# The state space branch and the convolutions of a hybrid trunk, scheduled ahead of the projections that run beside them

## The chip, the cores and the metric

The kernel runs on one core of a Trainium2 chip, as one program. Its engines are TensorE (PE for matmuls, PEld for their weight loads), VectorE (DVE), ScalarE (ACT), GpSimd (POOL) and SyncE (SP, which only starts transfers). Each engine has an instruction list of its own, fixed when the program is built; the engines are held together by semaphores. The metric is the device time of one execution in microseconds (us). Before the change it is 1503.3 us, the median of 3 runs (1502.55 to 1503.54).

## What is computed

A backbone of two layers over 256 latent tokens behind 256 context tokens, 512 tokens of width 1024 in all, in fp32. A conditioning vector gives shifts, scales and gates ("modulation"). Layer 0 mixes tokens with two parallel branches, a long convolution of order 2 on 768 channels and a diagonal state space model (S5) on 256 channels; layer 1 with a gated linear recurrence. Behind each stands a mixture of 32 experts.

```
def ab_mixer(h_lat, h_ctx, w_in, w_out, filt, conv_w, conv_b, hy_bias, s5p, ctx_out):
    ...
    p_lat = h_lat @ w_in
    u_lat = s5_in(p_lat)
    st_lf = s5_scan(u_lat, lam_bar[0], b_bar[0], st_cf[:, -1], False)
    st_lb = s5_scan(u_lat, lam_bar[1], b_bar[1], st_cb[:, 0], True)
    ...
    y = jnp.concatenate([hyena_mix(p[..., :3 * HY_D], filt, conv_w, conv_b, hy_bias),
                         s5_readout(u, st_f, st_b, c_mat, d, glu_w, glu_b)], axis=-1)
    return y.astype(p.dtype) @ w_out

def hyena_mix(u3, filt, conv_w, conv_b, bias):
    ...
    z = x1 * fft_conv(v, kf[:, 0], bias[0])
    return x2 * fft_conv(z, kf[:, 1], bias[1])
```

The in projection `w_in` is 1024 x 2560, the out projection `w_out` 1024 x 1024, the modulation of each layer 1024 x 6144.

## The kernel before

**Two kinds of work in layer 0.** `layer0_mixer` (L1214) traces layer 0's mixer as a main chain with work beside it, the *fill*.

The main chain has three parts. `tables()` (L1343) makes the S5 tables. `s5_mixer` (L793) and `s5_glu` (L830) are the state space branch: `s5_input` (L847) transposes the inputs `uT` by way of `UT` into `U`; then for each of four quarters of the groups `s5_quarter_tables` (L725) makes `Gt`, `Gm`, `Hm` and `Km`, `s5_state` (L870) multiplies `U` by `Gm`, rotates and scans on DVE and leaves `prev`, and three products per group (`Km` with `U`, `Hm` twice with `prev`) give the output. `Km` is laid out by eight small transfers from `KX` that ACT issues (L776). `convs()` (L1370) is the long convolution: for each of six units of 128 channels `hyena_spectra` (L935) makes the filter spectra `K`, and `hyena_unit` (L1025) does two convolutions, each a transform on PE (`zv` by `dft`), a stretch on DVE and POOL (`Z`, `t`, `Z`, `yy`) and the inverse transform on PE (8 products of `yy` and `dft`), whose result `zv` or `yo` is the next step's input.

The fill is a list of jobs that `pipeline` (L1175) runs a few matmuls at a time. `Inputs` and `Channels` (L1061) do the in projection of 128 columns: 24 matmuls of 512 columns (three products of split weights `whi`, `wlo` and split `h`), whose weights are split beforehand by ACT (`whi`) and POOL (`wlo`). `Mods` (L1113) do 512 columns of the modulation (16 matmuls of `sc` by `w`, then 4 transposes). `Out` (L1135) does 128 columns of the out projection for some of the channel blocks; it may be traced only when those units are done. All of them use the two PSUM banks `in`. The first list holds 12 in-projection jobs (4 steps each) and 10 modulation jobs (1 step each), 58 steps; the second the in projection of convolution units 0 to 3, the rest of the modulation and 32 out-projection jobs. The jobs of units 0 and 1 wait until the pool `hyzb` is opened, which is after S5 (L1362).

**What sets the order.** `drive` (L226) takes a step of the main chain, which yields a gap in us, and then traces fill steps until their costs cover the gap. That makes the order of tracing. From it the framework's scheduler makes each engine's list: it plays the program through in a model of the chip, and whenever an engine is free there, it takes, of the instructions whose inputs are ready, the one that was traced first. `E.first()` (L143) is `tc.high_priority(None)`: instructions traced inside it count as if traced at the program's start. In regions under `manual_schedule` the named engines keep the order of tracing among the region's own instructions; L1351 to 1353 (the first fill steps and `tables()`) is such a region for PE, while L1356, 1357 and 1387 are in none.

`tables()` yields over 80 gaps, each of which draws at least one fill step as long as there are any. So all 58 steps of the first list are traced before the first instruction of `s5_mixer`, and none is left to be traced between the steps of `s5_mixer` and `s5_glu`; the second list starts with `convs()`.

**Behind layer 0's mixer** `moe` (L1702) loads the expert weights (96 MB a layer) into pools that reuse the memory of the convolutions, routes the tokens and runs the experts; then comes layer 1 in the same way. Most operations are recorded at the helpers' lines: L165 matmul, L169 transpose, L172 ACT, L175 copy, L178 two-input elementwise, L181 scalar_tensor_tensor, L191 weight loads.

Of the kernel before, what the change touches and what calls it, by code (L numbers as in the profile page):

```python
# [2 lines left out]

# [1 line left out]

# [217 lines left out]
        yield  # L223


def drive(main, fill):  # L226


    for gap in main:
        while gap > 0:  # L230
            c = next(fill, None)
            if c is None:
                break
            gap -= c
# [558 lines left out]
def s5_mixer(E, o, ycat, tabs, hp, tp, wp):  # L793

    inp = []
    for m in range(2):
        if m == 0:
            Gm = next(tabs)
        inp.append((yield from s5_input(E, o, m, o.uT[:, m], wp, tp)))
    for m in range(2):  # L800
        U, ud = inp[m]
        y = o.uT[:, m].rearrange("p (g c) -> p g c", g=8)
        for i in range(2):
            q = 2 * m + i
            if q:
                Gm = next(tabs)
                yield 1.2
            sl = slice(4 * i, 4 * i + 4)
            prev = s5_state(E, o, q, U[:, sl], Gm, wp)
            yield 5.0  # L810
            Hm, Km = next(tabs)
            yield 4.5
            b = E.bank("s5")
            for g in range(4):
                oo = b[:, g * 64:(g + 1) * 64]
                E.mm(oo, Km[:, g, :], U[:, 4 * i + g, :], True, False)
                E.mm(oo, Hm[:, 0, g, :], prev[:, 0, g, :], False, False)
                E.mm(oo, Hm[:, 1, g, :], prev[:, 1, g, :], False, True)
            E.tt(y[:, sl], b[:, :256].rearrange("p (g c) -> p g c", c=64), ud[:, sl], ADD)
            if i == 1:  # L820
                yield 0.7
                yield from s5_output(E, m, y, ycat, tp)
            if q < 3:
                tabs = s5_quarter_tables(E, o, q + 1, hp, tp)
                next(tabs)
                yield 3.8
    E.dump('ys5', ycat[:, 6:8])


def s5_glu(E, ycat, tp):  # L830
    gw = tp.tile([P, 2, 512], F32, tag="Gt", name="gw")
    E.SY.dma_start(gw, E.a['s5_glu_w'][0].rearrange("(k p) n -> p k n", p=P))
    yield 0
    glb = E.prm['glb']
    ag = []
    for m in (2, 3, 0, 1):
        b = E.bank("s5")
        for k in range(2):
            E.mm(b, gw[:, k, m * P:m * P + P], ycat[:, 6 + k, :], k == 0, k == 1)
        ag.append(b)  # L840
    for m in range(2):
        sg = tp.tile([P, 512], F32, tag=f"t{'xy'[m]}", name="sg")
        E.act(sg, ag[m], AF.Sigmoid, bias=glb[:, 2 + m:3 + m])
        E.stt(ycat[:, 6 + m, :], ag[2 + m], glb[:, m:m + 1], sg, ADD, MUL)


def s5_input(E, o, m, uT, wp, tp):  # L847

    UT = tp.tile([64, 8, 8, 16], F32, tag="Gt", name="UT")
    uv = uT.rearrange("p (c j) -> p j c", j=8)  # L850
    for h in range(2):
        b = E.bank("s5")
        for i in range(4):
            E.tr(b[:64, i * P:(i + 1) * P], uv[:, 4 * h + i, :])
        E.copy(UT[:, :, 4 * h:4 * h + 4, :].rearrange("p g j n -> p j g n"),
               b[:64].rearrange("p (j g n) -> p j g n", j=4, g=8))
    yield 1.5
    U = wp.tile([P, 8, 64], F32, name="U", bufs=2)
    b = E.bank("s5")
    for g in range(8):  # L860
        E.tr(b[:, g * 64:(g + 1) * 64], UT[:, g].rearrange("p j n -> p (j n)"))
    bv = b.rearrange("p (g c) -> p g c", c=64)
    E.act(U[:, :, 0:32], bv[:, :, 32:64], AF.Copy)
    E.act(U[:, :, 32:64], bv[:, :, 0:32], AF.Copy)
    ud = wp.tile([P, 8, 64], F32, name="ud", bufs=2)
    E.tt(ud, U, bcast(o.dcol[:, 8 * m:8 * m + 8], 2, 64), MUL, E.G)
    return U, ud
# [47 lines left out]
def s5_output(E, m, y, ycat, tp):  # L915
    E.act(y, y, AF.Gelu_apprx_tanh)
    yield 0.8
    YT = tp.tile([64, 8, 8, 16], F32, tag="Gt", name="YT")
    for h in range(2):
        b = E.bank("s5")  # L920
        for i in range(4):
            E.tr(b[:64, i * P:(i + 1) * P], y[:, 4 * h + i, :])
        E.copy(YT[:, :, 4 * h:4 * h + 4, :].rearrange("p j g n -> p g j n"),
               b[:64].rearrange("p (g j n) -> p g j n", g=4, j=8))
    yield 1.5
    b = E.bank("s5")
    for j in range(8):
        E.tr(b[:, j * 64:(j + 1) * 64], YT[:, j].rearrange("p g n -> p (g n)"))
    bv = b.rearrange("p (j s c) -> p s c j", j=8, s=2)
    yv = ycat[:, 6 + m, :].rearrange("p (s c j) -> p s c j", s=2, j=8)  # L930
    E.act(yv[:, 1], bv[:, 0], AF.Copy)
    E.act(yv[:, 0], bv[:, 1], AF.Copy)
# [242 lines left out]
def pipeline(jobs):  # L1175


    now, late = 0.0, []

    def settle():  # L1180
        for x in list(late):
            while x[0] <= now:
                d = next(x[1], None)
                if d is None:
                    late.remove(x)
                    break
                x[0] = now + d

    jobs = iter(jobs)
    cur = next(jobs, None)  # L1190
    prepared = False
    while cur:
        while not cur.ready():
            yield None
        if not prepared:
            cur.prep()
        nxt = next(jobs, None)
        prepared = False
        for cost in cur.mms():
            if nxt and not prepared and nxt.ready():  # L1200
                nxt.prep()
                prepared = True
            settle()
            now += cost
            yield cost
        late.append([now, cur.after()])
        cur = nxt
    while late:
        now = max(now, min(x[0] for x in late))
        settle()  # L1210
        yield 0.4


def layer0_mixer(E):  # L1214
    class O:
        pass
    o = O()
# [6 lines left out]
    with ExitStack() as l0:  # L1224
        E.psum(l0, "left", **{"in": (1, 2), "tr": (1, 1)})
        pl = l0.enter_context(E.pool("p_l0", 1))
        ycat = pl.tile([P, KD, T], F32, name="ycat")
# [8 lines left out]
        hp = E.hp = s5s.enter_context(E.pool("s5h", 1, "right"))  # L1236
        tq = E.tq = s5s.enter_context(E.pool("s5t", 1, "right"))
# [76 lines left out]
        def more():  # L1314
            yield from first
            yield from jobs
            yh.extend(p_h.tile([P, KD, T], F32R, tag=f"h{i}", name=f"yh{i}") for i in range(2))
            for ks in ((4, 5, 6, 7), (0, 1), (2,), (3,)):
                for i in range(8):
                    yield Out(E, feed, i, ks, yh, ycat, tmp, lambda ks=ks: done.issuperset(ks), tail if ks[0] == 3 else None)  # L1320
                if ks[0] in (4, 0):
                    yield between.pop(0)
                    yield between.pop(0)
# [16 lines left out]
        fill = pipeline(more())  # L1340
        tabs = s5_quarter_tables(E, o, 0, hp, tq)
# [11 lines left out]
            drive(tables(), fill)  # L1353
        s5a.close()
        wp = s5s.enter_context(E.pool("s5w", 1, "right"))
        drive(s5_mixer(E, o, ycat, tabs, hp, tq, wp), fill)  # L1356
        drive(s5_glu(E, ycat, tq), fill)
        done.update((6, 7))
        s5s.close()
        hys = ExitStack()  # L1360
# [1 line left out]
        with hys, E.pool("hyzb", 2, "right") as zb, E.pool("hyk", 2, "right") as kp, E.pool("hyt", 1, "right") as tp, \  # L1362
                E.pool("hyw", 2, "right") as wp:
            zp.update({u: zb for u in (0, 1)})
            E.dft = zb.tile([P, 8, P], F32, name="dft", bufs=1)
            E.SY.dma_start(E.dft, a['k_dft'])
            order = (4, 5, 0, 1, 2, 3)
            filt = {}

            def convs():  # L1370
                for _ in hyena_spectra(E, 4, hdn2, kp, tp, filt):
                    yield 3.0
                for i, u in enumerate(order):
                    if i == 5:
                        tags = {"wge": ("fw3", 512), "bge": ("win", 256), "wA": ("hw", 1024), "lT": ("so", 512)}
                        ends["r"] = Route(E, 0, T // P, E.mT[0], lambda nm: tp.tile([P, tags[nm][1]], F32, tag=tags[nm][0], name=nm))
                        ends["r"].prepare(E.bank("hs")[:, 0])
                    spec = hyena_spectra(E, order[i + 1], hdn2, kp, tp, filt) if i < 5 else iter(())
                    steps(spec, 1)
                    while ("x1", u) not in zt:  # L1380
                        next(fill)
                    yield from hyena_unit(E, u, *filt[u], zt["v", u], zt["x1", u], ycat, wp, spec)
                    done.add(u)
                    run(spec)
                    yield 0.5

            drive(convs(), fill)
            run(fill)
    E.dump('ycat', ycat)
    E.dump('x1', E.xT)  # L1390
# [736 lines left out]
```

## Time and profile before

| | us |
|---|---|
| median of 3 runs | 1503.3 |
| the profiled execution's own time | 1504.8 |
| its span, first to last instruction | 1502.9 |
| PE busy | 1284.4 (85%) |
| DVE, ACT, POOL busy | 809.8, 381.9, 381.4 |
| mean granted TensorE clock | 0.925 |

Layer 0's mixer takes the first 530 us: the first list of the fill runs until 163, S5 until 274, the convolutions until 506, the last out projections and the norm until 530. The first mixture of experts takes 530 to 870. In the profile a busy PE at granted clock 1.0 runs at 2.4 GHz, at 0.5 at 1.2 GHz; a stretch with a mean between had both. Times in rows are us from the span's start.

### The profile page before, as it was taken

The page shows a single profiled execution, that of the slowest core. Times are in us where ns is not written, and L with a number is a line of the kernel's source. Part 1 is how long each engine was busy: PE and PEld are TensorE (multiplying, and loading weights), DVE is VectorE, ACT ScalarE, POOL GpSimd, SP SyncE. Part 2 cuts the span into 40 slices and gives each one's busy share as a digit, 9 for nine tenths or more (in the row PEclk, how much of TensorE's full clock was granted, in tenths as well). Part 3 has the DMA queues.
Part 4 walks back from the last instruction along what each step waited for, and adds up shares of the span by engine and source line. Part 5 has one row for each costly group of instructions (what it writes and reads, how often), then busy time and mean ns, then how long its engine had stood idle before and what let it go on. Part 6 is the DMA issues. An engine that isn't in the chain of part 4 may idle for free. (4 is left out here: it accounts for less than half of the span.)

```text
span 1502.9 us, 18344 instructions
## 1 busy us (share of the span) xinstructions
PE 1284.4 (85%) x6921; PEld 823.2 (55%) x6921; DVE 809.8 (54%) x1828; ACT 381.9 (25%) x644; POOL 381.4 (25%) x268
## 2 busy tenths in 40 slices
PE   5799698998888749999999487979798959999995
PEld 1566476566655433444444177878787733444443
DVE  4973364477776462444334687474747463444433
ACT  2323232222222321111111242333333212222211
POOL 0343343124544521111100342323232121111001
PEclk9899788898988869999999788999999979999998
DMA  9357533323032089999996102030303279999980
GB/s 380 148 197 281 201 122 95 124 74 120 14 111 84 29 333 379 412 384 372 380 388 239 65 8 113 29 112 29 113 28 120 96 316 376 417 418 417 419 330 31
DMA packets 54591, 311.88 MB, mean 208 GB/s; under 512 B 13239, under 2 KB 18648, under 8 KB 23128
## 3 DMA queue, kind: packets, MB, share of 16 engines
q1 hardware_dynamic: 47032, 302.68, 50.8%
q0 software_dynamic: 4608, 6.30, 1.3%
q10 hardware_dynamic: 2848, 1.58, 0.5%
q8 instruction: 59, 0.97, 0.3%
q14 instruction: 44, 0.36, 0.1%
HBM read 315.77 MB, written 4.19 MB: 213 GB/s over the span
## 5 line engine op out<-in xcount | busy, mean ns | idle before, releaser
L165 PE MATMUL pg_t<-w,Xe 128*64 128x512 f32 x1024 | 228.8, 600 | 0.0
L165 PE MATMUL in_t<-h,whl 128*128 128x512 f32 (+1 forms) x768 | 146.6, 349 | 3.2 <-DVE h L175 2.4
L165 PEld LDWEIGHTS pg_t<-w,Xe 128*64 128x64 f32 x1024 | 71.1, 138 | 135.7 <-issue 131.1
L178 POOL TENSOR_TENSOR whl<-wraw,whl 128x2048 fp32r<-128x2048 f32 x20 | 93.5, 4680 | 175.3 <-ACT whl L172 175.3
L165 PEld LDWEIGHTS in_t<-h,whl 128*128 128x128 f32 x768 | 122.3, 197 | 20.9 <-POOL h L178 3.1
L165 PE MATMUL in_t<-h,whi 128*128 128x512 f32 x320 | 112.4, 431 | 17.0 <-ACT whi L172 7.8
L165 PE MATMUL py_t<-w,hid 128*64 128x512 f32 x512 | 119.1, 606 | 4.2 <-DVE yl L178 3.0
L181 DVE SCALAR_TENSOR_TENSOR sg<-sg,ws,pg_t 128x256 f32<-128x256 f32 x32 | 15.4, 480 | 181.2 <-ACT sg L172 181.2
L181 DVE SCALAR_TENSOR_TENSOR xT<-sc_t,mT,xT 128x256 f32<-128x256 f32 x204 | 90.3, 480 | 29.6 <-PE sc_t L165 28.1
L178 POOL TENSOR_TENSOR wlo<-w,whi 128x1024 fp32r<-128x1024 f32 (+3 forms) x51 | 74.1, 1458 | 126.8 <-ACT whi L172 119.3
L1547 POOL MEMSET Xg<- 128x1024 f32 x32 | 30.4, 958 | 297.4 <-PE ga_t L169 297.3
L165 PE MATMUL sc_t<-OT,yh 128*128 128x512 f32 (+1 forms) x256 | 90.7, 369 | 10.1 <-DVE xT L181 7.8
L165 PEld LDWEIGHTS in_t<-h,whi 128*128 128x128 f32 x320 | 62.7, 205 | 36.6 <-issue 9.3
L165 PE MATMUL sc_t<-OT,yl 128*128 128x512 f32 (+1 forms) x256 | 82.6, 338 | 0.0
L165 PEld LDWEIGHTS sc_t<-OT,yh 128*128 128x128 f32 x256 | 48.1, 188 | 54.1 <-issue 27.6
L165 PEld LDWEIGHTS py_t<-w,hid 128*64 128x64 f32 x512 | 34.1, 138 | 64.8 <-issue 55.9
L165 PE MATMUL in_t<-h,wlo 128*128 128x512 f32 x160 | 68.4, 427 | 1.2 <-POOL wlo L178 1.1
L172 ACT ACTIVATE yh<-py_t 128x1024 fp32r<-128x1024 f32 (+1 forms) x34 | 33.1, 973 | 121.0 <-PE py_t L165 121.0
L185 DVE TENSOR_SCALAR OT<-ht_t,ksq 128x512 fp32r<-128x512 f32 (+1 forms) x32 | 19.7, 617 | 81.5 <-PE ht_t L165 81.5
L172 ACT ACTIVATE sg<-pg_t 128x256 f32<-128x256 f32 x32 | 12.3, 384 | 195.6 <-PE pg_t L165 195.6
L172 ACT ACTIVATE whi<-w 128x1024 fp32r<-128x1024 f32 (+3 forms) x52 | 34.4, 664 | 103.4 <-PE in_t L165 83.2
L165 PE MATMUL at_t<-QA,X 128*128 128x128 f32 x224 | 37.2, 316 | 26.9 <-DVE QA L178 26.9
(411 smaller groups left out, 2378.0 us busy)
## 6 DMA issues: line engine op xcount, KB each, us to landing
w<-in_w_gu_dram SPq DMA_DIRECT2D x128, 1024.0 KB, 10.4
w<-in_w_dn_dram SPq DMA_DIRECT2D x64, 1024.0 KB, 10.2
w<-in_w_mod_dram SPq DMA_DIRECT2D x24, 2048.0 KB, 7.9
wraw<-in_w_in_dram SPq DMA_DIRECT2D x20, 1024.0 KB, 5.6
w<-in_w_in_dram SPq DMA_DIRECT2D x5, 2048.0 KB
w<-in_w_out_dram SPq DMA_DIRECT2D x2, 2048.0 KB
cwo<-in_w_out_dram SPq DMA_DIRECT2D x2, 2048.0 KB
rows<-hh SPq DMA_DIRECT2D x6, 512.0 KB, 2.6
```

The costliest lines, as they stand in the source:

```text
L165: self.TE.matmul(o, l, r, start=st, stop=sp)
L172: self.S.activation(o, i, f, **k)
L178: (e or self.V).tensor_tensor(o, x, y, op=op)
L181: self.V.scalar_tensor_tensor(o, x, s, y, op0=op0, op1=op1)
L185: (e or self.V).tensor_scalar(o, x, s1, None, op0=op0)
L1547: E.G.memset(X, 0.0)
```

## The change

`drive` gets a third parameter. Where it is given, each step of the main chain is traced inside `E.first()`, and the fill steps as before. Three of the four calls give it: S5, its gated output, and the convolutions; the call for `tables()` does not. Nothing that is computed changes, nor the order of tracing, nor any buffer.

```diff
-def drive(main, fill):
-
-
-    for gap in main:
+def drive(main, fill, E=None):
+
+
+    while True:
+        with E.first() if E else nullcontext():
+            gap = next(main, None)
+        if gap is None:
+            return
         while gap > 0:
             c = next(fill, None)
             if c is None:
@@ -1353,8 +1357,8 @@
-        drive(s5_mixer(E, o, ycat, tabs, hp, tq, wp), fill)
-        drive(s5_glu(E, ycat, tq), fill)
+        drive(s5_mixer(E, o, ycat, tabs, hp, tq, wp), fill, E)
+        drive(s5_glu(E, ycat, tq), fill, E)
@@ -1384,7 +1388,7 @@
-            drive(convs(), fill)
+            drive(convs(), fill, E)
             run(fill)
```

## Rows read from the trace of the kernel before

**Rows 1.** The page, parts 1 and 2: engines, and the granted clock in 40 slices.
```profile
PE 1284.4 (85%) x6921; PEld 823.2 (55%) x6921; DVE 809.8 (54%) x1828; ACT 381.9 (25%) x644; POOL 381.4 (25%) x268
...
PEclk9899788898988869999999788999999979999998
```
**Rows 2.** Windows of layer 0's mixer: stretch, length, busy by engine, PEclk, DMA, GB/s.
```profile
100.00:154.00 54.00, 53.86 (x326) 36.52 (x324) 19.50 (x44) 16.46 (x28) 20.27 (x14) 1.00 0.76 306
154.00:264.00 110.00, 88.92 (x601) 65.71 (x600) 51.42 (x92) 30.35 (x56) 39.88 (x27) 0.83 0.39 134
264.00:345.00 81.00, 73.83 (x316) 48.54 (x315) 50.98 (x109) 20.32 (x34) 23.61 (x16) 0.91 0.28 95
345.00:506.00 161.00, 128.85 (x572) 92.58 (x572) 108.84 (x223) 38.51 (x81) 71.36 (x61) 0.87 0.20 75
506.00:530.00 24.00, 20.31 (x125) 10.10 (x125) 9.35 (x27) 8.41 (x20) 13.97 (x16) 0.93 0.22 63
```
**Rows 3.** The same windows for PE's fill products alone (tile in_t).
```profile
100.00:154.00 54.00, 46.81 (x236) 1.00 0.76 306
154.00:264.00 110.00, 42.94 (x184) 0.83 0.39 134
```
**Rows 4.** Timeline of PE from 97 us: start, us, engine, line, operation, count.
```profile
98.25 0.60 PE L169 MATMUL s_t<-ksq,uT 128*64 128x128 f32 x4
...
105.43 1.92 PE L165 MATMUL in_t<-w,sc 128*32 128x512 f32 x16
107.28 0.65 PE L169 MATMUL s_t<-ksq,uT 128*64 128x128 f32 x4
...
143.77 1.55 PE L165 MATMUL s_t<-U,Gm 128*128 128x64 f32 x12
```
**Rows 5.** Timeline of POOL: the last Hm product of the first quarter.
```profile
104.37 1.29 POOL L178 TENSOR_TENSOR Hm<-ux,uy 128x512 f32<-128x512 f32 x1
```
**Rows 6.** Timeline of PE, first and second quarter's output (idle time before, releaser).
```profile
170.75 0.80 PE L165 MATMUL in_t<-h,whi 128*128 128x512 f32 x1 [7.35 <-ACT whi L172]
175.95 0.66 PE L165 MATMUL s_t<-U,Km 128*128 128x64 f32 x2 [4.40 <-DMA Km<-KX]
...
184.87 0.36 PE L165 MATMUL s_t<-Hm,wB 64*16 64x112 f32 x2
...
202.43 0.33 PE L165 MATMUL s_t<-U,Km 128*128 128x64 f32 x2
```
**Rows 7.** Timeline of ACT: transfers that ACT issues, and what stands behind them.
```profile
163.91 5.69 ACTq L777 DMA_DIRECT2D Km<-KX  x7
169.65 2.00 ACT L172 ACTIVATE whi<-w 128x1024 fp32r<-128x1024 f32 x2 [5.77 <-issue]
...
192.10 4.47 ACTq L777 DMA_DIRECT2D Km<-KX  x7
```
**Rows 8.** Timeline of DVE and POOL around 214 us.
```profile
213.41 0.68 DVE L178 TENSOR_TENSOR ty<-wB,PG 128x512 f32<-128x512 f32 x1
...
214.85 2.73 DVE L178 TENSOR_TENSOR tx<-wB,PG 128x512 f32<-128x512 f32 x1
...
214.62 2.41 POOL L178 TENSOR_TENSOR wlo<-w,whi 128x1024 fp32r<-128x1024 f32 x1 [1.68 <-ACT whi L172]
```
**Rows 9.** Timeline of PE in the last convolution unit.
```profile
481.02 1.19 PE L165 MATMUL pd_t<-yy,dft 128*128 128x256 f32 x2 [3.94 <-DVE yy L178]
...
490.36 0.59 PE L165 MATMUL pd_t<-yy,dft 128*128 128x256 f32 x2
...
500.44 3.56 PE L165 MATMUL pd_t<-yy,dft 128*128 128x256 f32 x8 [6.35 <-DVE yy L178]
```
**Rows 10.** Waits of PE from 264 to 506 us: total, times, longest.
```profile
PE pd_t L165 <- DVE yy L178: 13.3, 4, 6.3
```
**Rows 11.** Timeline of SP: routing weights, and expert weights behind the mixer.
```profile
441.53 0.58 SPq L1415 DMA_DIRECT2D wge<-in_moe_wg_dram  x1
...
466.64 61.94 SPq L1533 DMA_DIRECT2D w<-in_w_gu_dram  x4
```

More of the change, by code (lines that the diff above doesn't have):

```diff
@@ L1 @@
 import math
-from contextlib import ExitStack
+from contextlib import ExitStack, nullcontext
 import numpy as np
```

## The prediction

> **What bounds the kernel now.** I read the page first: PE is busy for 85% of the span, DVE, the next, for 54%, and its granted clock drops in places [rows 1]. A change to the order of layer 0's mixer can win only there, so the next view was the table of windows over that mixer. In 100 to 154 us PE is busy for 53.86 of 54 us at clock 1.00; in 154 to 264 for 88.92 of 110 at 0.83; from 264 to 506 for 202.7 of 242 at 0.91 and 0.87 [rows 2]. DVE reaches 68% at most, DMA is at 0.20 to 0.39 from 154 on. So the mixer is PE-bound while there is fill, and afterwards bound by the main chain's latency, with PE idle or slowed. Filtered to the fill's products, the first of these windows has 46.81 us of them in 54 and the second 42.94 in 110 [rows 3]: the fill is used up early.
>
> The timeline of PE shows why. In the dense stretch S5's pieces stand at 98.25, 107.28 and, three further ones left out, 143.77 us, about 9.1 apart, each directly behind a modulation product (such as the one at 105.43, 1.92 us long) [rows 4]. That is where the first list has nothing ready for a moment. The whole first list was traced before S5, so it goes first; S5 gets one slot a round. Its first quarter's output product comes at 175.95, after the list has ended, with PE waiting 7.35 and 4.40 us just before [rows 6].
>
> **The change part by part.** No instruction is added or removed; three drives move forward in the lists. I sum against the profiled execution, 1504.8 us; the median of the runs is 1.5 us less.
>
> *S5, seen from its own chain.* With priority its pieces take PE when their inputs are there. The earliest it can have its first Hm is when POOL has finished it, 104.37 + 1.29 = 105.7 us; that belongs to `tables()`, which gets no priority [rows 5]. From the first product on Hm to the output product the second quarter, which met little fill, took 202.43 - 184.87 = 17.6 us, including the Km transfers [rows 6]. So the first output product could stand at 105.7 + 17.6 = 123 instead of 176: 53 us. The later three quarters already had precedence, because what ran beside them was traced after S5, so they keep their pace and only move.
>
> On VectorE S5's two-input operations move into a stretch in which POOL splits weights. The row: a `tx` of the usual shape took 2.73 us beside a `wlo` of 2.41 that had begun 0.23 earlier, while the `ty` before it took 0.68 [rows 8]: 2.05 us lost. The 236 fill products from 100 to 154 us [rows 3] are about six projection jobs (24 each) with as many modulations (16 each), so six `wlo`: up to 12 us of the 53 may go, 41 remain. The Trainium skill, SBUF — State Buffer, section "Who interferes with whom", says that a VectorE instruction with two SBUF inputs and a GpSimd instruction that reads SBUF exclude each other, whichever starts first holding the shared ports; the trace agrees with this by the 2.73. By that rule the chain would give 41, without it 53; the sum below uses neither.
>
> *S5, seen from PE.* Moving S5 up doesn't make its products vanish. What can be won is PE's idle time, 110 - 88.92 = 21.1 us, plus the slow clock: a mean of 0.83 means that 34% of the 110 us, 37.4, ran at 1.2 GHz; at 81% busy that is 30.3 us of work that takes half as long at 2.4, 15.1 saved. Together 36.2. That is less than the 41, so I take it as the term, since in 100 to 154 the fill held PE at 99.7% and clock 1.00. From it go the stalls that ACT makes: for each quarter it issues eight Km transfers, seven of them in 5.69 or 4.47 us, and the fill's weight splits stand behind them (5.77 us of idle ACT before `whi`) [rows 7]. PE waited 7.35 for that at the first quarter, when it had nothing else [rows 6]; in the dense stretch a running job covers most of it. Bounds per quarter: 0 and 7.35; I take 0.8, the nearer end because two `in` banks hold a job ahead, so 3.2 for four. S5 term: 33.0.
>
> *The convolutions.* An inverse transform is eight products. In the last unit the first was cut up by out projections: from 481.02 to 490.36 + 0.59, 9.93 us; the second stood alone and took 3.56 [rows 9]. Twelve such groups exist (two per unit). With priority they run in one piece. The last unit is on the path that sets the end, since only the last block of out projections is behind it: 9.93 - 3.56 = 6.4 us, and the work that is pushed aside fits into the 6.35 us that PE waits before the second group. For the other units the gain lies between 0 (the fill displaced has to be done anyway) and PE's idle time and slow clock in 264 to 506: 39.3 us idle, and by the same arithmetic 6.6 and 16.8 of clock, 62.7. I take 0 for them, as the row of a group without fill before it is from the last unit. Convolution term: 6.4.
>
> *Transfers.* The moved steps also issue the Km transfers on ACT (32, counted above), the load of the gate weights, two loads for each unit's filter and four routing loads on SP. They pass the weight loads of the fill on SP. Each takes SP about 0.58 us [rows 11] and DMA is mostly idle there; if a weight load had to wait for one, 0.6 us of a ring with three tiles ahead: nothing. On POOL a quarter's `Hm` products (1.29 each) [rows 5] go ahead of `wlo`; that is in the bounds of the starved rival.
>
> *What is late next.* Everything behind the mixer moves with its end. The expert weights reuse the convolutions' memory: three more of the four loads that start at 466.64 wait until 528.6 for it [rows 11]; they follow the mixer, and no wait of theirs stands still. The 24 us from 506 to 530 stay.
>
> Sum: 33.0 + 6.4 = 39.4. 1504.8 - 39.4 = 1465.4 in a profiled execution, 1464 as a median.
>
> **The rivals.**
>
> *The fill is starved.* ACT and POOL serve S5 first, and PE waits for `whi` and `wlo` in every quarter as at 170.75: 4 x 7.35 = 29.4 us. Of the 36.2 + 6.4 there remain 13.2: 1490. For it: the ACT row with 5.77 us idle. Against: at the second quarter the same transfers cost PE no such wait.
>
> *More than PE's stage shows.* S5 wins its full 53 and the fill that is left over goes into the idle time of the convolutions, where the last unit and one more win 6.4 each: 53 + 13 = 66, 1437. For it: 39.3 us of idle PE there. Against: the port rows above.
>
> *It doesn't do what it says.* In the scheduler's model S5 was not ready earlier either, for the shared tiles `Gt`/`UT` hold it, or the lists come out in nearly the same order: 1503. For it: one buffer for both. Against: pieces exactly behind each modulation product are the mark of a low rank, not of a late input.
>
> *Slower: PE's list waits at its head.* One mechanism: a main product now stands in PE's list where the model has its input ready, with no fill in front; if DVE and POOL are later on the chip, all of PE's list waits. Where no fill stood before it, the last inverse group waited 6.35 us; four such groups together 13.3 [rows 9, 10]. If all twelve wait 5 us, that is 60, 46.7 more than now, against the 33 of S5: 14 slower, 1517. It decides from (33 + 13.3) / 12 = 3.9 us a group. The Trainium skill, PSUM — Partial Sum Buffer, section "Engine vs sequencer instructions", says that matmuls start and complete in program order; the 6.35 us agree, since out projections were traced behind. Against: most groups wait less now, and eight of twelve not at all, though fill is low in the convolutions already.
>
> **How the numbers follow.** Forecast 0.50 (its own range 1446 to 1482: 53 for 36 on one side, the stalls on the other), starved 0.18, more 0.10, nothing 0.07, slower 0.15. Predicted 1464. A range from 1436 to 1504 leaves out the slower case and the far end of "more", about 0.18. The measurement tells 0.2%, 3 us, from no change: faster 0.78, same 0.07, slower 0.15.
>
> **What would show it.** In the changed kernel's trace: the transposes of `UT` and the products of `U` and `Gm` before 115 us and no longer one per modulation product; `U,Km` first at about 123 to 135; the gated output at about 235 to 240 instead of 272; the fill's products in 154 to 264 rising from 43 towards 65 us and the clock there above 0.95; inverse groups of eight in one piece; the first large run of expert loads near 489 instead of 529. Wrong, if the first `U,Km` stays behind 160, if PE's wait for ACT `whi` or POOL `wlo` grows to over 20 us between 100 and 264, or if its waits for `yy` exceed 45 us: then the gain is eaten where the rivals say.

## The result, and the profile after

The changed kernel takes 1522.8 us (1520.9 to 1530.7) against 1503.2: ratio 1.0141 [1.0103, 1.0179], slower by 1.4%, where 1464 was predicted. Its profiled execution took 1524.7 us, span 1522.9. On the page, PE's busy time grew by 18.6 us with the same number of products [rows 1]; in the third and fourth of the 40 slices (76 to 152 us) the granted clock is 0.7 for 0.9.
```profile
span 1522.9 us, 18342 instructions
...
PE 1303.0 (86%) x6921; PEld 825.7 (54%) x6921; DVE 825.4 (54%) x1828; ACT 381.7 (25%) x644; POOL 380.2 (25%) x268
...
PEclk9977889899887878999999979999999979999998
```
The windows of the mixer, all engines:
```profile
100.00:154.00 54.00, 44.00 (x257) 27.57 (x256) 30.06 (x47) 13.29 (x28) 26.98 (x22) 0.78 0.36 127
154.00:264.00 110.00, 95.52 (x562) 61.36 (x560) 48.76 (x103) 29.62 (x49) 26.54 (x19) 0.91 0.41 153
264.00:345.00 81.00, 73.37 (x347) 53.15 (x347) 53.92 (x108) 20.52 (x33) 28.79 (x17) 0.94 0.37 137
345.00:506.00 161.00, 138.68 (x594) 96.74 (x593) 107.18 (x194) 37.25 (x72) 64.01 (x51) 0.86 0.23 83
506.00:530.00 24.00, 15.48 (x71) 8.21 (x68) 6.66 (x18) 9.42 (x25) 12.19 (x18) 0.86 0.46 175
```
The same windows for PE's fill products (tile in_t):
```profile
100.00:154.00 54.00, 21.64 (x81) 0.78 0.36 127
154.00:264.00 110.00, 48.27 (x220) 0.91 0.41 153
264.00:345.00 81.00, 43.09 (x179) 0.94 0.37 137
345.00:506.00 161.00, 75.41 (x299) 0.86 0.23 83
506.00:530.00 24.00, 13.10 (x53) 0.86 0.46 175
```
The dense stretch is gone: from 100 to 154 us there are 81 fill products for 236 and the clock is 0.78 for 1.00 [rows 2, 3]. The later windows make up for it bit by bit: 220 for 184, then 179 for 120, 299 for 248, and behind 506 us 53 for 24.

S5 did move. The timeline of PE (last field: idle time before, and who ended it) has the first quarter's products on Hm from 105, its output product at 128 (before: 175.95 [rows 6]), and pauses where S5 heads the list and GpSimd's Hm is not there:
```profile
105.31 0.56 PE L165 MATMUL s_t<-Hm,wB 64*16 64x112 f32 x8 [1.33 <-POOL Hm L178]
105.80 1.04 PE L165 MATMUL in_t<-w,sc 128*32 128x512 f32 x2
109.72 0.55 PE L165 MATMUL s_t<-Hm,wB 64*16 64x112 f32 x2 [2.88 <-POOL Hm L178]
...
114.51 3.43 PE L165 MATMUL in_t<-w,sc 128*32 128x512 f32 x14
...
128.32 0.41 PE L165 MATMUL s_t<-U,Km 128*128 128x64 f32 x2 [1.98 <-DMA Km<-KX]
...
137.68 0.36 PE L165 MATMUL s_t<-Hm,wB 64*16 64x112 f32 x2 [2.98 <-POOL Hm L178]
```
The second pause cuts a modulation in two: two of its 16 products run at 105.80, and the other 14, whose weights are there, only at 114.51, behind the wait for `Hm` and S5's products.

The end of the mixer, as ACT and DVE show it: the last unit's copy `yo`, the last two modulations' copies `ms`, and the multiplication that finishes a unit (`ycat`).
```profile
498.40 0.60 ACT L172 ACTIVATE yo<-pd_t 128x512 f32<-128x512 f32 x1 [8.28 <-PE pd_t L165]
...
506.11 0.60 ACT L172 ACTIVATE ms<-in_t 128x512 f32<-128x512 f32 x1 [1.01 <-PE in_t L165]
...
517.44 0.60 ACT L172 ACTIVATE ms<-in_t 128x512 f32<-128x512 f32 x1 [7.42 <-PE in_t L165]
...
520.30 0.88 DVE L181 SCALAR_TENSOR_TENSOR ycat<-tr_t,nv,ycat 128x256 f32<-128x256 f32 x2 [0.83 <-PE tr_t L169]
```
And PE in the same stretch, with SP's issue of the load that PE waits for:
```profile
448.08 3.23 PE L165 MATMUL pd_t<-yy,dft 128*128 128x256 f32 x8 [2.36 <-DVE yy L178]
...
504.12 1.92 PE L165 MATMUL in_t<-w,sc 128*32 128x512 f32 x16
...
506.10 0.33 SPq L191 DMA_DIRECT2D w<-in_w_mod_dram  x1
...
514.00 3.37 PE L165 MATMUL in_t<-w,sc 128*32 128x512 f32 x16 [5.55 <-DMA w<-in_w_mod_dram]
...
519.63 0.63 PE L169 MATMUL tr_t<-ksq,yo 128*128 128x128 f32 x4
...
537.77 0.40 PE L165 MATMUL in_t<-yh,wlo 128*128 128x512 f32 x1
```
`yo` is ready at 498.40 but is transposed at 519.63. Its transposes take the one `tr` bank, whose uses follow the order of tracing; the last modulations were traced earlier, so their transposes have it first. They are late: the last one's products wait 5.55 us for a weight load that SP issued at 506.10, as the products of the one before ended. Before, the modulations were done first, and the last `yo` went straight through:
```profile
476.26 0.60 ACT L172 ACTIVATE ms<-in_t 128x512 f32<-128x512 f32 x1 [2.09 <-PE in_t L165]
...
504.03 0.60 ACT L172 ACTIVATE yo<-pd_t 128x512 f32<-128x512 f32 x1 [10.17 <-PE pd_t L165]
...
505.46 0.88 DVE L181 SCALAR_TENSOR_TENSOR ycat<-tr_t,nv,ycat 128x256 f32<-128x256 f32 x2 [4.57 <-PE tr_t L169]
...
519.52 0.40 PE L165 MATMUL in_t<-yh,wlo 128*128 128x512 f32 x1
```
Behind the last out-projection product (519.5 before, 537.8 after) the rest of the span is 983.4 and 985.1 us: of the 20.0 us that the profiled span grew by, 18.3 are lost in the mixer.

### The profile page after: what moved, and what is told of

Read it like the earlier page. It is cut to its first block, busy times and chain, and to the rows that moved or that the text cites. A ratio compares the mean times of both kernels' runs of the same rounds, so it can differ in the third digit from the quotient of the medians.

```text
span 1522.9 us, 18342 instructions
## 1 busy us (share of the span) xinstructions
PE 1303.0 (86%) x6921; PEld 825.7 (54%) x6921; DVE 825.4 (54%) x1828; ACT 381.7 (25%) x644; POOL 380.2 (25%) x268
## 5 line engine op out<-in xcount | busy, mean ns | idle before, releaser
L165 PE MATMUL in_t<-w,sc 128*32 128x512 f32 x384 | 67.2, 696 | 8.4 <-DMA w<-in_w_mod_dram 8.4
```

The source lines that it names most:

```text
L165: self.TE.matmul(o, l, r, start=st, stop=sp)
```

## The experiments

Each ratio is against the kernel before. The table has start times from each profiled execution: the gated output (`G`), the last projection's copy (`zx`), the last unit's `yo`, the last modulation's `ms`, the last out-projection product (`Out`); then `Out` minus `yo`, which I call the tail, and PE's products counted in 100 to 264 us (a few records can be missing, and the expectations below have 924, 813 and 794 where the table has 925, 817 and 792).

| kernel | G | zx | yo | ms | Out | tail | products | ratio [interval] |
|---|---|---|---|---|---|---|---|---|
| before | 272 | 367 | 504.0 | 476.3 | 519.5 | 15.5 | 925 | |
| changed | 239 | 399 | 498.4 | 517.4 | 537.8 | 39.4 | 817 | 1.0141 [1.0103, 1.0179] |
| e1 S5 only | 241 | 371 | 506.7 | 478.6 | 522.3 | 15.6 | 784 | 1.0044 [1.0027, 1.0061] |
| e2 convolutions only | 270 | 364 | 476.0 | 493.7 | 514.4 | 38.4 | 927 | 0.9973 [0.9954, 0.9993] |
| e3 changed, own bank | 246 | 453 | 469.5 | 525.7 | 545.8 | 76.3 | 790 | 1.0180 [1.0143, 1.0217] |
| e4 changed, evictions first | 242 | 397 | 496.4 | 515.6 | 535.9 | 39.5 | 801 | 1.0132 [1.0096, 1.0167] |
| e7 changed, tables on DVE | 245 | 401 | 500.0 | 518.9 | 539.5 | 39.5 | 786 | 1.0111 [1.0070, 1.0152] |
| e8 convolutions by 60 | 268 | 362 | 505.2 | 487.7 | 521.3 | 16.1 | 919 | 1.0050 [1.0034, 1.0067] |
| e9 = e2, modulations early | 268 | 363 | 475.9 | 435.2 | 498.4 | 22.5 | 936 | 0.9893 [0.9857, 0.9929] |
| e10 = changed, modulations early | 243 | 404 | 492.0 | 454.1 | 514.5 | 22.5 | 792 | 0.9980 [0.9961, 0.9998] |
| e11 = before, modulations early | 268 | 362 | 501.8 | 423.6 | 518.8 | 17.0 | 932 | 1.0026 [1.0011, 1.0040] |
| e12 = e9, own bank | 267 | 352 | 472.5 | 445.2 | 497.5 | 25.0 | 928 | 0.9886 [0.9851, 0.9921] |
| e13 = e9, S5 by 150 | 279 | 373 | 486.5 | 445.8 | 509.0 | 22.5 | 897 | 0.9929 [0.9899, 0.9958] |
| e14 = e10 + e4 + e7 | 246 | 402 | 490.1 | 452.3 | 512.4 | 22.3 | 810 | 0.9951 [0.9930, 0.9971] |
| e15 = e9, S5 by 400 | 247 | 387 | 475.1 | 436.9 | 498.7 | 23.6 | 871 | 0.9886 [0.9857, 0.9915] |

**One part at a time.** e1 takes the priority from the convolutions, e2 from S5 and its gated output.
```
e1:  drive(convs(), fill)
e2:  drive(s5_mixer(...), fill);  drive(s5_glu(...), fill)
```


> Priority for S5 alone; the convolutions as before. Theory A (S5 on VectorE puts off the evictions that free the fill's PSUM banks, the fill starves in 100 to 154 us, and that costs the time): 1515 to 1525 us, and the fill's products in 100 to 154 us stay near 22 us. Theory B (the loss is in the convolutions, whose outputs wait for the tr bank behind the fill): faster than before, 1470 to 1490, since the gated output still stands at about 238 us. Theory C (PE's list waits at its head for DVE and POOL): 1495 to 1505.

> Priority for the convolutions alone; S5 as before. Theory A: no loss is left, 1495 to 1504 us. Theory B: most of the loss is here, 1513 to 1525, with 20 us or more from a unit's last ACT copy (yo) to its ycat. Theory C: 1510 to 1520 with PE's waits for yy and hw above 30 us in 264 to 530.

No theory met both numbers (A met e2's; B's sign, 20 us from `yo` to `ycat`, came in e2, but not its loss). S5 alone costs 0.44%, 6.6 us, where theory A wanted 12 to 22, and its gated output 31 us earlier gives a last `yo` 2.7 us later. The convolutions alone win 0.27%, 4.1 us; yet their last `yo` is 28 us earlier. The tail takes 22.9 of that back. The two parts add up to 0.2%, and together they cost 1.4%: most of the loss arises only where both go ahead of the fill. The rows of e2, with the same order of events as in the changed kernel:
```profile
476.04 0.60 ACT L172 ACTIVATE yo<-pd_t 128x512 f32<-128x512 f32 x1 [7.23 <-PE pd_t L165]
...
490.14 3.51 PE L165 MATMUL in_t<-w,sc 128*32 128x512 f32 x16 [5.50 <-DMA w<-in_w_mod_dram]
...
496.59 0.88 DVE L181 SCALAR_TENSOR_TENSOR ycat<-tr_t,nv,ycat 128x256 f32<-128x256 f32 x2 [0.83 <-PE tr_t L169]
```
**The bank, and the evictions.** e3 gives a unit's output transposes a `pd` bank; e4 puts the three evictions of a projection at the priority of S5.
```
e3:      yield 0.8
-    b = E.bank("tr")
+    b = E.bank("pd")
e4:  in Channels.after
+    with E.first():
         E.act(y, ...); E.stt(yv[:, :, 1:], ...); E.stt(yv[:, :, :255], ...)
```


> The changed kernel, but a convolution unit's output transposes take a pd bank, which the fill never holds, instead of the tr bank. Theory A: the fill is late all the same, 1515 to 1523 us. Theory B: yo to ycat falls from 20 to 60 us a unit to under 4, and the time to 1495 to 1505. Theory C: 1520 to 1525.

> The changed kernel, but the projection's three evictions (one ACT, two DVE) have the same priority as the steps of S5. Theory A: the fill's products in 100 to 154 us rise from 21.6 to over 35 us and the time falls to 1480 to 1503. Theory B: no change, 1518 to 1525. Theory C: slower yet or no change, 1520 to 1530, as three more instructions a job go ahead of S5's.

No theory met e3's time. B and C both met e4's, which changed nothing; B's other sign came in e3 (`ycat` 1.6 us behind `yo`), without the gain, and C's waits did not come (below). With its own bank the main chain runs 29 us further ahead (`yo` 469.5) and the fill falls back further (last projection 453 for 399), so that the end is 8 us later: the wait for the bank seems to have been a brake that let the fill through. Evictions first leave the fill of 100 to 154 us at 21.88 us (x75). It was not late evictions that kept it out.

**Less fill.** Modulations take half of their contraction and projections leave out the third product, so the values differ from the reference, in both kernels alike.
```
-    for k in range(KD):                     (modulation, fill jobs only)
+    for k in range(4):
-    mm3(E, self.b, self.w, self.hT, (k, k + 1), ...)
+    for i in (k, k + 1): for h in range(2): E.mm(self.b, self.w[0][:, i, :], self.hT[h][:, i, :], ...)
```


> The changed kernel with less fill: a modulation product takes half of its contraction, a projection leaves out its third product (low half of the weights), so the values differ. It stands against e6, the kernel before with the same cut. Theory F (in the changed kernel the fill, pushed back, sets the mixer's end; the main chain really is ahead): without so much fill the main chain sets it, and e5 is 15 to 40 us faster than e6. Theory W (the prioritised steps wait at the head of PE's list, so that the main chain gains nothing over the whole mixer): e5 is as slow as e6 or up to 20 us slower.

> The kernel before with the cut of e5. About a third of the fill's products is gone, but S5's and the convolutions' chains stay: theory F 1470 to 1495; theory W the same, as the two differ only in e5.

1799.6 and 1792.7 us; the changed values route the experts otherwise (1536 products in the experts' first matmul for 1024), so only the two can be compared. e5 is 6.9 us slower, and theory F misses. Theory W's figure fits, its mechanism doesn't. In e5:
```profile
466.74 0.60 ACT L172 ACTIVATE yo<-pd_t 128x512 f32<-128x512 f32 x1 [8.12 <-PE pd_t L165]
...
481.18 1.94 PE L165 MATMUL in_t<-w,sc 128*32 128x512 f32 x8 [5.82 <-DMA w<-in_w_mod_dram]
...
487.30 0.88 DVE L181 SCALAR_TENSOR_TENSOR ycat<-tr_t,nv,ycat 128x256 f32<-128x256 f32 x2 [1.32 <-PE tr_t L169]
```
In e6:
```profile
483.85 0.60 ACT L172 ACTIVATE yo<-pd_t 128x512 f32<-128x512 f32 x1 [10.01 <-PE pd_t L165]
...
485.28 0.88 DVE L181 SCALAR_TENSOR_TENSOR ycat<-tr_t,nv,ycat 128x256 f32<-128x256 f32 x2 [4.70 <-PE tr_t L169]
```
The main chain is 17 us ahead, and the unit is finished 2 us later: even with a third of the fill gone the last modulation sets the end. That points not to the amount of fill but to where its last jobs stand; e9 and e10 test it.

**S5's tables on VectorE; a smaller step.** e7 takes GpSimd out of Hm; e8 moves the convolutions by 60 places, S5 not at all.
```
e7:  E.tt(ux, x[0], y[0], MUL)  ... (six, without E.G)
e8:  with E.first(60) if E else nullcontext():
```


> The changed kernel, with the six products of each S5 quarter that make Hm on VectorE instead of GpSimd. If PE's waits for GpSimd's Hm at the head of its list (8.4 us in four waits, and the clock behind them) break the dense stretch: fill's products in 100 to 154 us from 21.6 to over 30 us, clock there from 0.78 to over 0.9, and 1500 to 1512 us. If the fill is held by something else: waits for Hm gone, the window's fill within 3 us of 21.6, and 1515 to 1525.

> The kernel before, with the convolutions' steps alone moved forward by 60 places in the list instead of to its start. Theory F: the last unit's output is earlier than before (504 us) but the last modulations not as late as with full priority (494), so 1492 to 1499, better than e2 (1499.8). If the convolutions' gain is only their own pace: 1500 to 1503.

In e7 the clock of 100 to 154 us is 0.90 and the fill there 23.44 us; the time stays at 1522.8, as the second expectation had it. PE no longer waits for `Hm`, but in 100 to 264 us it is idle for 26.8 us (24.5 without the edit): other waits took their place, the longest 6.1 us for the load of `dft`. So GpSimd's tables alone decide nothing. e8 (1511.3) misses both figures and is the worst of both: the modulations come later (487.7 for 476.3), the last unit doesn't come earlier (505.2).

**The tail moved.** Between the first eight out projections, one modulation behind every second; before, two followed these and two the next eight.
```
     for i in range(8):
         yield Out(...)
+        if ks[0] == 4 and i % 2:
+            yield between.pop(0)
-    if ks[0] in (4, 0):
-        yield between.pop(0)
-        yield between.pop(0)
```


> e2 (priority for the convolutions alone), with the last four modulations one behind every second job of the first block of out projections instead of two behind the first block and two behind the second. Theory T (the fill's tail is a chain of its own: out projections, then modulations whose weight load waits for the one before, then the shared banks; with the main chain first this chain sets the end): the last unit's ycat, 21 us behind its yo in e2, comes within 8 us, the mixer ends 10 to 20 us earlier, 1480 to 1492 us. Theory P (the amount of the fill's work beside the convolutions sets the end, in whatever order): 1497 to 1503.

> The changed kernel with the modulations moved as in e9. Theory T: 1500 to 1512 us, the out projections' last product at 515 to 528 instead of 537.8. Theory P: 1518 to 1525.

> The kernel before with the modulations moved as in e9, no priority. Both theories: the main chain sets the end here (its last yo stands at 504, the last modulation at 476), so no gain, 1500 to 1510; what e9 wins over e2 is then not the move by itself.

> e9 with a unit's output transposes on a pd bank. Theory T: the wait of ycat for the fill's use of the tr bank is what is left, a further 0 to 6 us, 1476 to 1490. Theory P: slower than e9, as the main chain runs further ahead of the fill (e3 against the changed kernel: 8 us), 1498 to 1510.

Theory T's ranges hold in e9, e11 and e12; e10 is 1.3 us better than its range (1498.7, last product at 514.5). In e9 the last unit goes straight through:
```profile
475.89 0.60 ACT L172 ACTIVATE yo<-pd_t 128x512 f32<-128x512 f32 x1 [6.23 <-PE pd_t L165]
...
477.33 0.88 DVE L181 SCALAR_TENSOR_TENSOR ycat<-tr_t,nv,ycat 128x256 f32<-128x256 f32 x2 [3.16 <-PE tr_t L169]
```
The tail is 22.5 us for 38.4 in e2, and e9 beats the kernel before by 1.1%; without priority the same move costs 0.26% (e11), and the bank adds nothing (e12). In the changed kernel the move takes the loss away: 1.0141 becomes 0.9980 (e10). But e10 is 12.7 us slower than e9, and they differ only in S5's priority.

**How early S5.** e13 and e15 are e9 with S5 moved by 150 and 400 places; e14 is e10 with the edits of e4 and e7.
```
e13, e15:  with E.first(n) ...  n = 150 / 400 for s5_mixer and s5_glu, None for convs
```


> e9 (convolutions with priority, modulations early), with S5's steps moved forward by 150 places, where e10 has them at the list's start. Theory D (in 100 to 264 us PE gets through fewer products the earlier S5 stands in its list: 924 before, 813 with full priority; no S5 step that is early is worth that): little of the dense stretch is given up, 1483 to 1491 us, so no better than e9 (1486). Theory L (S5 early is worth its 25 us, and only the waits behind GpSimd and VectorE eat it): 1474 to 1483.

> As e13 with 400 places. Theory D: between e9 and e10, 1488 to 1498, and the count of products in 100 to 264 us between theirs. Theory L: 1470 to 1483, better than e13.

> e10 (full priority for S5 and the convolutions, modulations early) with both helpers: S5's Hm on VectorE (e7) and the projection's evictions at the same priority (e4). Theory D: no help, 1493 to 1503. Theory L: those two waits were what ate S5's gain, 1475 to 1488, and over 870 products in 100 to 264 us (e10 had 794).

PE from 100 to 264 us in e9, e15 and e10 (the count in brackets is of products, long and short alike):
```profile
100.00:264.00 164.00, 141.44 (x936) 0.93 0.52 193
```
```profile
100.00:264.00 164.00, 151.51 (x871) 0.88 0.46 169
```
```profile
100.00:264.00 164.00, 144.82 (x792) 0.80 0.39 143
```
The further forward S5 is put, the fewer products PE finishes there, though it is busy as long or longer, at a lower clock. Theory D holds for e14 (1495.5) and for the count. It misses the times of e13 (1493.6, outside) and e15 (1486.3, better than it said): at 400 places S5 is 22 us earlier than in e9 and the last `yo` only 0.8, so nothing is lost, nothing won. Theory L misses all three. Why 150 places do worse than 400 (gated output at 279 us, later than without priority) I can't say; that stays open.

## Why the prediction was wrong

- *S5's pace: right.* First output product at 128.3 (123 to 135 forecast), gated output at 238.5 (235 to 240).
- *S5's worth: the step that failed.* The term of 33 us won was 6.6 us lost in e1. It took PE's idle time and slow clock in 154 to 264 us as room for the fill that S5 displaces, and let the dense stretch stay "at 99.7% and clock 1.00" with S5 put into it. But the fill is slower beside S5 than nearly alone. Nearly alone it went at 236 / 54 = 4.4 products per us [rows 3]; beside S5 with priority at 81 / 54 = 1.5, then 220 / 110 = 2.0. So idle time and slow clock were not used up but came over into the dense stretch: in 100 to 264 us PE was idle for 21.2 us before and for 10.0 + 14.5 = 24.5 after, and by the prediction's own arithmetic 37.4 us before and 54 x 0.22 x 2 + 110 x 0.09 x 2 = 43.6 after ran at 1.2 GHz. The fill in 154 to 264 rose to 48 us, not 65, and the clock there to 0.91, not above 0.95. From 54 us to the last out-projection product PE carries out the same work in the kernel before, e1, e9 and e10 (in this order: length, busy, clock):
```profile
54.00:519.52 465.52, 394.70 (x2044) 0.89 0.33 122
54.00:522.26 468.26, 403.70 (x2037) 0.88 0.33 121
54.00:498.40 444.40, 381.95 (x2044) 0.93 0.35 127
54.00:514.52 460.52, 403.23 (x2043) 0.90 0.34 123
```
The term's two halves were 21.1 us of idle time and 15.1 us of slow clock, both to be won in 154 to 264 us; these lines show what became of each by the end. S5's priority alone (e1 against before) took away 6.3 us of idle time, but PE was busy 9.0 us longer with the same products; beside the convolutions' (e10 against e9) it was 5.2 and 21.3. So the first half was too large and the second had the wrong sign. These are single executions, and busy time that fills what would have been a wait costs nothing: the sums tell what grew, not why. The Trainium skill, PSUM — Partial Sum Buffer, section "Engine vs sequencer instructions", says that matmuls start and complete in program order; the trace agrees where S5 heads PE's list (2.88 us behind `Hm` before 109.72, with 14 products of a modulation ready behind it), but e7 shows that this wait alone is not what decides. The 6.35 us that the prediction took for agreement can't show it: the out projections behind that group needed the output of its own unit.
- *Where the 34 us went.* Units 4 and 5, the first two, keep them (`yo` at 288.4 and 313.4, before at 316.2 and 352.9). Then the main chain meets the fill it overtook: the next unit's `zx`, done at 260.5 before, comes at 316.8, the last projection is done at 399 us for 367, and the last `yo` is 5.6 us early. The price of S5's priority, measured: +6.6 us alone, about +25 in the changed kernel against e2 (1.0141 and 0.9973), +12.7 in e10 against e9, 0 at 400 places; a gain in none.
- *The convolutions: near the number by luck.* 6.4 us forecast, 4.1 measured, but as the difference of two sizes that the prediction did not have. Their chain won 28 us and not 6.4, and "the 24 us from 506 to 530 stay" was wrong: 15.5 us of tail became 38.4. Under *Transfers* I priced a weight load at "nothing" by the ring's depth; the last one is waited for 5.55 us.
- *Rivals.* The starved fill was right in kind, not in its cause: in 100 to 264 us the waits of PE list neither `whi` nor `wlo`. The slower rival came near the time (1517) by another mechanism: PE's waits for `yy` did not grow from 13.3 us [rows 10] towards 60 but fell:
```profile
PE hs_t L165 <- DVE hw L178: 7.0, 3, 3.2
PE pd_t L165 <- DVE yy L178: 6.7, 3, 3.7
PE hs_t L165 <- DVE dg L185: 6.6, 4, 4.1
PE in_t L165 <- DMA w<-in_w_mod_dram: 5.6, 1, 5.6
```
(264 to 546 us). None of the three signs of being wrong came (`U,Km` at 128, no wait for `whi` or `wlo`, 6.7 us for `yy`), and none of my rivals had the path change from the main chain to the fill, which is what e2 and e9 show.
- *Not settled:* what holds PE below its dense rate beside S5. The evictions (e4) and GpSimd's tables (e7) are not it, together worth some 3 us (e14 against e10, intervals overlapping). Nor is it settled why the same products kept PE busy longer: the clock is 0.03 lower in e10 than in e9, but only 0.01 in e1 than before.

## What to carry to other kernels

Where two streams share an engine, write down when each ends before giving one the precedence. Here the last modulation had 28 us of slack (476.3 against a last `yo` at 504.0); in e2 the convolutions moved 28 us forward and it moved 17 us back, so that the overtaken stream's last jobs, with their serial loads and the shared bank, became the path. Work displaced from a dense stretch is to be priced at the rate that it reaches beside the chain, not at its rate alone. The convolutions' priority paid properly only once the order of tracing (which buffers follow whatever the priority) was changed with it: 0.27% became 1.1%.

## What the runs showed of the hardware

Sixteen modulation products took 1.92 us at 504.12 and 3.37 us at 514.00. PE's granted clock in these stretches, and in the pause between (length, busy, clock, DMA):
```profile
504.10:506.10 2.00, 1.94 (x17) 1.00 0.03 8
506.10:514.00 7.90, 1.41 (x9) 0.75 0.86 336
514.00:517.40 3.40, 3.40 (x17) 0.57 0.34 145
```
PE had been busy for 1.41 of the 7.9 us before, and the products then ran at 0.57, nearer 1.2 than 2.4 GHz: the wait of 5.55 us cost a further 1.45.
